# Loading and norming x in two groups around the first conditioning half, with the engines pinned in program order

## The chip, the cores and the metric

The kernel runs on one core of a Trainium2 chip. The metric is the time of one execution on the device, in microseconds; several runs are made and their median is given. One more execution is recorded by the profiler, and all positions below ("at 59.68") are microseconds from the start of the span in that record. The engines are TensorE (PE, with its weight loads as PEld), VectorE (DVE), ScalarE (ACT), GpSimd (POOL) and SyncE (SP), which here only issues transfers.

## The reference

One inference step of a small decoder trunk with two layers, width 1024, for a prompt of 1024 tokens and 8 single decode tokens. Each sub-layer normalises, modulates by a conditioning vector, runs a mixer or an FFN, and adds the gated result:

```python
def modulate(x, g, shift, scale):
    y = rms_norm(x, g) * (1.0 + scale[:, None, :]) + shift[:, None, :]
    return y.astype(x.dtype)

def ada_params(c, w, b):
    return (jax.nn.silu(c) @ w + b).astype(jnp.float32)

# in trunk(), for each layer l
sh1, sc1, g1, sh2, sc2, g2 = jnp.split(ada_params(c, w_ada[l], b_ada[l]), 6, axis=-1)
xn = modulate(h, norm_w[l, 0], sh1, sc1)
# layer 0: hgrn2_mixer(xn, ...), 8 heads, q, f_raw, i, g = split(xn @ w_in)
# layer 1: attention over a window of 128, with sinks and a shared K/V
h = h + g1 * mix
xn = modulate(h, norm_w[l, 1], sh2, sc2)
h = h + g2 * swiglu(xn, w_ffn_in[l], w_ffn_out[l])
```

So before the first product of layer 0 the kernel needs three things: the transposed input, the root mean square of each token, and the first 2048 columns of the conditioning product (shift and scale). All of it is float32.

## The kernel before

Activations lie transposed in SBUF: eight tiles `h[k]`, 128 features by 1024 tokens, and a small tile `hd` for the eight decode tokens. The 1032 tokens are cut into three chunks of 344 columns (grid `G3`). Every product in full precision is made of three matmuls on rounded float32 (`mm3`, lines 283 to 285): operands are split into a rounded high part and a low rest, and high by high, high by low and low by high are added in PSUM. A weight tile comes by a transfer into `raw` (line 195), ScalarE rounds it (line 182) and POOL subtracts to get the rest (line 185). For the first four units of weights this conversion is not run at once but kept in `held` and called by hand with `held.pop(0)()`.

The start, in the order in which it is written:

- SyncE loads the conditioning vectors, then the eight x blocks of 128 tokens (`load_x`, line 382), the first weight unit, eight row tiles of 512 KB of the first conditioning half (`first_half`, line 401), two more weight units, and then the second half.
- ScalarE squares and sums each x block (`first_square`, line 863). TensorE transposes the blocks in three groups (`turn_x`, line 455) and VectorE copies them into `h` (line 457).
- All nine columns of sums go through one reciprocal root (`newton`, lines 543 to 552). VectorE writes the results on diagonals (line 893), and TensorE spreads them over all partitions with a matrix of ones (line 909) into `N.R` (line 910).
- `first_step` (line 503) multiplies the conditioning vectors with the row tiles, eight steps for a half. `first_end` copies the sums (line 514), transposes them (line 517) and makes shift and scale (lines 522 and 523, and 530 in `mod_scale`). A half serves four of the eight feature tiles.
- `Norm.apply_steps` makes the input of the products: VectorE multiplies `h`, scale and `N.R` (line 740), ScalarE adds the shift and rounds (line 744), VectorE takes the rest (line 745).
- `hgrn_first` makes the four products of head 0. With the first half alone, parts of 12 matmuls over four feature tiles can run (`part(c, i)` for chunk `c`, unit `i`). Then come the second conditioning half, the applies that it frees, and the full products (288 matmuls in all). The written order has parts (0,0), (0,1), (0,2), (1,0), the eight steps of the second half, part (1,1), its end, and part (1,2).

PSUM has two pools of four banks, `mmp()` (mm) and `axp()` (ax). A tile with tag `c4` takes one of 34 slots in SBUF.

The order on each engine comes from a scheduler with a model of times. It may move an instruction ahead of others on its engine when it takes the inputs to be there. `tc.keep_in_program_order(i)` pins an instruction behind the one written before it on its engine. In the kernel before, only a few instructions are pinned. So the loads of the attention sinks (lines 1261 and 1266) and the copies of the K and V caches (lines 1269 and 1270), which are written in `biases()` and called in the middle of the first FFN, are issued within the first 65 us. `biases()` also negates the sinks on VectorE (line 1272, pinned).

Of the kernel before, what the change touches and what calls it, by code (L numbers as in the profile page):

```python
# [11 lines left out]
AF = mybir.ActivationFunctionType  # L12
ALU = mybir.AluOpType
# [4 lines left out]
P = 128  # L18
D = 1024
KT = 8  # L20
# [45 lines left out]
def trunk_kernel(  # L66
# [203 lines left out]
    def ada_unit(w, k, c0):  # L270
# [9 lines left out]
        ca.add(go)  # L280

    def mm3(ps, wh, wl, xh, xl, first, last):
        pe.matmul(ps, wh, xh, start=first, stop=False)  # L283
        pe.matmul(ps, wh, xl, start=False, stop=False)  # L284
        pe.matmul(ps, wl, xh, start=False, stop=last)  # L285

# [93 lines left out]
    def load_x(tb):  # L380
        t = big(cols=D)
        sp.dma_start(t, x_prompt[0, tb * P : (tb + 1) * P, :])
        xt.append(t)
# [10 lines left out]
    act.dma_start(pr2[56:57, :], gnorm_a)  # L394
    for tb in range(3, 8):
        load_x(tb)


# [7 lines left out]
    for kk in range(4):  # L406
        t = big(cols=1024)
        wa[0].append(first_half(2 * kk, 0, t))
        t = big(cols=1024)
        wa[0].append(first_half(2 * kk + 1, 0, t))  # L410
    ws.ahead(3)
    for k in range(4):
        t = big(cols=1024)
        wa[1].append(first_half(k, 1, t))

# [34 lines left out]
    dve.tensor_copy(hd, ps[:, : KT * NB].rearrange("p (k b) -> p k b", k=KT))  # L450
    def turn_x(t0, n):
        for k in range(KT):
            ps = mmp() if k % 2 else axp()
            for j in range(n):
                pe.transpose(ps[:, j * P : (j + 1) * P], xt[t0 + j][:, k * P : (k + 1) * P], ident)
            dst = h[k][:, t0 * P : (t0 + n) * P]
            dve.tensor_copy(dst, ps[:, : n * P])


# [22 lines left out]
    def ada_end(q):  # L482
# [7 lines left out]
        for b in range(4):  # L490
# [5 lines left out]
            )  # L496

    def first_step(i, k):
        if k == 0:
            ada_ps[0] = axp()  # L500
        for s in range(2):
            j = s + 2 * (k % 2)
            pe.matmul(
                ada_ps[0][32 * j : 32 * j + 32, :],
                cT[:, k, :],
                wa[i][k][:, s * 512 : (s + 1) * 512],
                start=(k < 2),
                stop=(k >= KT - 2),
                tile_position=(0, 32 * j),
            )  # L510

    def first_end(i):
        a = big(cols=512)
        act.copy(a, ada_ps.pop(0))
        ps = axp()
        for b in range(4):
            pe.transpose(ps[:, b * P : (b + 1) * P], a[:, b * P : (b + 1) * P], ident)
# [4 lines left out]
        dve.tensor_tensor(dst, psv[:, 0:2, :, 0:9], bc(bias, 3, 9), op=ALU.add)  # L522
        dve.tensor_tensor(dst, dst, psv[:, 2:4, :, 0:9], op=ALU.add)
        mod_scale(0, ks)

    MODS = {0: (0, 8, 0), 1: (24, 32, 8), 2: (96, 104, 32), 3: (48, 56, 16), 4: (72, 80, 24)}

    def mod_scale(m, ks=slice(0, KT)):
        _, sc, nw = MODS[m]
        dve.scalar_tensor_tensor(  # L530
            modA[:, m, ks, :],
            ada[:, sc : sc + KT, :][:, ks, :],
            1.0,
            bc(nT[:, nw : nw + KT][:, ks], 2, 9),
            op0=ALU.add,
            op1=ALU.mult,
        )
# [144 lines left out]
    class Norm:  # L682
# [50 lines left out]

        def apply_steps(self, c, m, x):
            sh = MODS[m][0]
            n, s = self.g.pl[c], self.g.prompt(c)
            for k in range(KT):
                xh, xl = (z[:, :n] for z in x.at(k, self.g, c))
# [123 lines left out]
    def first_square(tb):  # L862
        act.activation(junk[:, :T], xt[tb], AF.Square, accum_out=ms[:, tb : tb + 1])

    act.activation(junk[:NB, :T], xd_in, AF.Square, accum_out=ms[:NB, 8:9])
    for tb in range(3):
        first_square(tb)
    turn_x(0, 3)
    for tb in range(3, 6):
        first_square(tb)  # L870
    turn_x(3, 3)
    for tb in range(6, 8):
        first_square(tb)
    held.pop(0)()


# [11 lines left out]

    dve.tensor_scalar(ms, ms, 1.0 / D, EPS, op0=ALU.mult, op1=ALU.add)
    newton(y, ms, 9, P, "n")  # L890
    for half in range(2):
        s = slice(512 * half, 512 * half + 512)
        dve.tensor_tensor(
            dg[:, s].rearrange("p (j q) -> p j q", j=4),
            bc(ident, 1, 4),
            bc(y[:, 4 * half : 4 * half + 4], 2, P),
            op=ALU.mult,
        )
    dve.tensor_tensor(dg[:NB, T:TOK], ident[:NB, :NB], y[:NB, 8:9].to_broadcast([NB, NB]), op=ALU.mult)
    turn_x(6, 2)  # L900
    for k in range(4, KT):
        wa[1].append(first_half(k, 1, big(cols=1024)))
    ws.ahead(4)
    for k in range(2):
        first_step(0, k)
    for half in range(2):
        s = slice(512 * half, 512 * half + 512)
        ps = axp()
        pe.matmul(ps, ones, dg[:, s], start=True, stop=True)
        act.copy(N.R[:, s], ps)  # L910
    ps = axp()
    pe.matmul(ps[:, :NB], ones[:NB, :], dg[:NB, T:TOK], start=True, stop=True)
    act.copy(N.R[:, T:TOK], ps[:, :NB])
    for k in range(2, KT):
        first_step(0, k)
    first_end(0)
    X = Rows(KT)
    steps = [N.apply_steps(c, 0, X) for c in range(NCH)]
    held.pop(0)()
    for c in range(2):  # L920
        for _ in range(2):
            next(steps[c])
        if c == 0:
            held.pop(0)()
# [40 lines left out]
    def hgrn_first():  # L965
# [3 lines left out]
        def part(c, i):  # L969
            acc[c, i] = axp() if c and i < 2 else mmp()  # L970
            proj(acc[c, i][:, :W], us[i], X, c, 0, 4)

        for c, i in ((0, 0), (0, 1), (0, 2), (1, 0)):
            part(c, i)
        for k in range(KT):
            first_step(1, k)
        part(1, 1)
        first_end(1)
        part(1, 2)
        held.pop(0)()  # L980
        for st in steps:
            for _ in st:
                pass
        for _ in us:
# [258 lines left out]
    def biases():  # L1243
# [16 lines left out]
        sk = cst.tile([P, 16], F32, name="sk")  # L1260
        sp.dma_start(sk, sinks_b[0].partition_broadcast(P))
        skd = cst.tile([P, 1], F32, name="skd")
        late = cst.tile([P, 2 * P], F32, tag="early", name="late")
        biasd = late[:, 0:P]
        for b in range(NB):
            sp.dma_start(skd[16 * b : 16 * b + 16, :], sinks_b[0].unsqueeze(1))
            sp.dma_start(biasd[16 * b : 16 * b + 16, 1:P], rd[:, P : 2 * P - 1])
            sp.dma_start(biasd[16 * b : 16 * b + 16, 0:1], rd[:, 2 * P - 1 : 2 * P])
        sp.dma_start(ck_sample[:, 0 : WIN - 1], cache_swa_k[:, 1:WIN])
        sp.dma_start(cv_sample[:, 0 : WIN - 1], cache_swa_v[:, 1:WIN])  # L1270
        for t in (sk, skd):
# [788 lines left out]
```

## Time and profile before

| what | value |
|---|---|
| median of 3 runs | 2515.46 us (2510.66 to 2519.86) |
| time of the profiled execution | 2514.68 us |
| its span, first to last instruction | 2512.9 us |
| TensorE busy | 2462.7 us, 98% of the span |
| VectorE, ScalarE, POOL busy | 1388.1, 898.8, 789.8 us |
| mean granted TensorE clock | 0.993 |
| TensorE idle, waiting on a last conditioning row | 1.8 us ahead of 28.89 |
| first `mm3` matmul | at 39.42 |
| first matmul behind the second conditioning half | at 59.68 |

A line of a timeline reads: start, duration, engine, source line, operation, output and input tile names, shapes, count of merged instructions, and in brackets the idle time before it with what ended it. Tiles with tag `c4` are called `c`. Instructions of one engine can overlap by about a tenth of a microsecond, so the distance of two starts tells more of a stream's rate than a duration does.

### The profile page before, as it was taken

What the parts mean: (1) busy time and instruction counts of PE and PEld (TensorE: products, weight loads), DVE (VectorE), ACT (ScalarE), POOL (GpSimd) and SP (SyncE); (2) the same over time, 40 slices, a digit from 0 to 9 for tenths busy, and PEclk for the clock granted to TensorE, in tenths of its full rate; (3) what the DMA queues carried; (4) which work ended last, traced back from release to release, by engine and by line L of the source; (5) the groups of instructions that cost most, each with busy time, mean ns of one, the idle gap of its engine ahead of it and who ended that gap; (6) DMA issues with size and microseconds to landing.
All of it is one profiled execution on the core that took longest, in us unless ns stands there. A gap on an engine that the chain in (4) does not pass through costs nothing.

```text
span 2512.9 us, 52301 instructions
## 1 busy us (share of the span) xinstructions
PE 2462.7 (98%) x21531; PEld 2338.6 (93%) x21531; DVE 1388.1 (55%) x3153; ACT 898.8 (36%) x2003; POOL 789.8 (31%) x575
## 2 busy tenths in 40 slices
PE   7999999999999999999999999999999999999998
PEld 5999999987889999999999997878999999999998
DVE  5544544454587554656433735576875555565436
ACT  4433333331363332333211555454543333333112
POOL 1211111120325444544432130202254444445221
PEclk9999999999999999999999999999999999999999
DMA  8564222258942223226321322433222222264201
GB/s 313 194 207 147 73 80 70 76 150 269 289 126 85 78 85 120 89 84 233 127 71 56 93 56 60 140 105 110 76 85 77 76 77 77 76 236 144 68 26 68
DMA packets 314560, 293.41 MB, mean 117 GB/s; under 512 B 28681, under 2 KB 291738, under 8 KB 314290
## 3 DMA queue, kind: packets, MB, share of 16 engines
q1 hardware_dynamic: 313920, 289.86, 35.9%
q8 instruction: 169, 2.77, 0.5%
q14 instruction: 69, 0.57, 0.1%
q10 hardware_dynamic: 402, 0.22, 0.0%
HBM read 231.27 MB, written 63.99 MB: 117 GB/s over the span
## 4 chain that ended last, share of the span: by engine, by line
PE 90%; DVE 4%; DMA 2%; issue 2%; ACT 1%; SPq 0%; ACTq 0%; POOL 0%; DVEq 0%; POOLq 0%
PE mm L283 21%; PE mm L284 20%; PE mm L285 20%; PE ax L283 6%; PE ax L285 6%; PE ax L284 6%; PE ax L473 2%; PE ax L1806 1%; PE ax L1877 1%; PE ax L1045 1%; PE ax L1863 1%; PE ax L1135 1%; PE ax L1172 1%; PE ax L1171 0%; DMA gd<-rd 0%
## 5 line engine op out<-in xcount | busy, mean ns | idle before, releaser
L185 POOL TENSOR_TENSOR wu<-raw,wu 128x512 fp32r<-128x512 f32 x464 | 632.3, 1370 | 1429.5 <-ACT wu L182 1313.4
L283 PE MATMUL mm<-c,wu 128*128 128x344 f32 (+1 forms) x2096 | 670.3, 320 | 5.4 <-ACT c L744 4.3
L284 PE MATMUL mm<-c,wu 128*128 128x344 f32 (+1 forms) x2096 | 658.7, 314 | 0.1
L285 PE MATMUL mm<-c,wu 128*128 128x344 f32 (+1 forms) x2096 | 658.5, 314 | 0.0
L182 ACT CAST wu<-raw 128x512 fp32r<-128x512 f32 x464 | 285.5, 620 | 678.6 <-PE mm L285 363.7
L283 PEld LDWEIGHTS mm<-c,wu 128*128 128x128 f32 x2096 | 395.7, 189 | 18.5 <-issue 9.3
L284 PEld LDWEIGHTS mm<-c,wu 128*128 128x128 f32 x2096 | 396.1, 189 | 4.2 <-issue 3.4
L285 PEld LDWEIGHTS mm<-c,wu 128*128 128x128 f32 x2096 | 395.6, 189 | 2.5 <-issue 2.4
L283 PE MATMUL mm<-xq,wu 128*128 128x258 f32 x1376 | 391.3, 284 | 1.3 <-ACT wu L182 1.0
L285 PE MATMUL mm<-xq,wu 128*128 128x258 f32 x1376 | 389.6, 283 | 0.8 <-POOL wu L185 0.8
L284 PE MATMUL mm<-xq,wu 128*128 128x258 f32 x1376 | 389.9, 283 | 0.0
L283 PE MATMUL ax<-xq,wu 128*128 128x258 f32 x1120 | 316.7, 283 | 0.0
L285 PE MATMUL ax<-xq,wu 128*128 128x258 f32 x1120 | 316.3, 282 | 0.0
L284 PE MATMUL ax<-xq,wu 128*128 128x258 f32 x1120 | 316.1, 282 | 0.0
L283 PEld LDWEIGHTS mm<-xq,wu 128*128 128x128 f32 x1376 | 260.9, 190 | 2.7 <-ACT wu L182 1.2
L285 PEld LDWEIGHTS mm<-xq,wu 128*128 128x128 f32 x1376 | 261.0, 190 | 2.3 <-issue 1.2
L284 PEld LDWEIGHTS mm<-xq,wu 128*128 128x128 f32 x1376 | 261.8, 190 | 0.1
L846 DVE SCALAR_TENSOR_TENSOR hs<-mm,ada,hs 128x344 f32<-128x344 f32 (+3 forms) x228 | 120.6, 533 | 179.1 <-PE mm L285 170.4
L284 PEld LDWEIGHTS ax<-xq,wu 128*128 128x128 f32 x1120 | 212.0, 189 | 0.0
L283 PEld LDWEIGHTS ax<-xq,wu 128*128 128x128 f32 x1120 | 211.6, 189 | 0.0
L285 PEld LDWEIGHTS ax<-xq,wu 128*128 128x128 f32 x1120 | 211.3, 189 | 0.0
L846 DVE SCALAR_TENSOR_TENSOR c<-mm,ada,c 128x344 f32<-128x344 f32 (+1 forms) x132 | 75.0, 571 | 111.9 <-PE mm L285 111.7
(323 smaller groups left out, 3633.8 us busy)
## 6 DMA issues: line engine op xcount, KB each, us to landing
c<-in_w_ada_dram SPq DMA_DIRECT2D x96, 512.0 KB, 7.8
raw<-in_w_ffn_in_dram SPq DMA_DIRECT2D x160, 256.0 KB, 3.2
ff<-c SPq DMA_DIRECT2D x44, 516.0 KB, 2.7
c<-ff SPq DMA_DIRECT2D x44, 516.0 KB, 7.8
raw<-in_w_ffn_out_dram SPq DMA_DIRECT2D x44, 512.0 KB, 3.5
raw<-in_w_in_a_dram SPq DMA_DIRECT2D x32, 512.0 KB, 4.4
hs<-hs SPq DMA_DIRECT2D x16, 516.0 KB, 4.4
out_dram<-c SPq DMA_DIRECT2D x16, 512.0 KB, 3.3
```

The lines of the kernel that those rows point to most:

```text
L182: i = act.copy(u[:, 0, :], src)
L185: eng.tensor_tensor(u[:, 1, :], src, u[:, 0, :], op=ALU.subtract)
L283: pe.matmul(ps, wh, xh, start=first, stop=False)
L284: pe.matmul(ps, wh, xl, start=False, stop=False)
L285: pe.matmul(ps, wl, xh, start=False, stop=last)
L473: pe.matmul(ada_ps[q][32 * j : 32 * j + 32, 256 * i : 256 * i + 256], cT[:, k, :], u[i][:, j, :], start=(k == 0 and i == 0), stop=(k == KT ...
L846: dve.scalar_tensor_tensor(hc, ps[:, : g.pl[c]], ada[:, gate + n, 0:1], hc, op0=ALU.mult, op1=ALU.add)
L1045: pe.matmul(ps[32 * j : 32 * j + 32, c * 32 : (c + 1) * 32], KS[:, t0 : t0 + 32], QP[:, t0 : t0 + 32], start=True, stop=True, tile_positio ...
L1135: pe.matmul(ps[:, j * P : (j + 1) * P], kt[:, s], vt[:, s], start=True, stop=True)
L1172: pe.matmul(o, attT[:, c, :], vt[:, s], start=(c == 0), stop=True)
L1806: pe.matmul(psv[hf][:, gi, s0:256], q[2 * gp + gi][r, tb * P : (tb + 1) * P], kT[a][r, (tb - 1) * P + s0 : (tb + 1) * P], start=True, stop ...
L1863: pe.transpose(ps[:, g * P : (g + 1) * P], L[:, g, sb * P : (sb + 1) * P], ident)
```

## The change

The diff does five things.

1. Loading: only three x blocks are loaded ahead of the first conditioning half. The other five come after it and after the second weight unit. All eight row tiles of the second half are issued behind the fourth weight unit.
2. Norming in two groups: the first three blocks (384 tokens, enough for chunk 0) are squared, transposed, rooted and spread around the steps of the first half. The other five blocks and the decode column follow behind the first two parts of head 0, in `hgrn_first`. The copies of blocks 6 and 7 go to ScalarE.
3. Applying: for feature tiles 0 to 3, `first_scaled` multiplies `h` and `N.R` before shift and scale are known. `first_apply` then uses scale and shift at once on ScalarE, and on VectorE makes the unrounded value again and subtracts. Tiles 4 to 7 of chunk 0 go the same way; the rest still goes through `apply_steps`, with a new argument for the first tile.
4. Order: nearly every instruction of this stage on TensorE, ScalarE and VectorE is pinned (`fix`), the parts of head 0 by the flag `in_order`. The full products are not pinned. The parts are now (0,0), (0,1), then the second norm group, (0,2), (0,3), applies of chunk 1, (1,0), four steps of the second half, (1,1), four more steps, and the end of the half.
5. In `biases()` the sink loads and the cache copies are pinned on SyncE's queue, in the middle of the first FFN.

```diff
     def mm3(ps, wh, wl, xh, xl, first, last):
+        def put(i):
+            if in_order[0]:
+                tc.keep_in_program_order(i)
...
-    for tb in range(3, 8):
-        load_x(tb)
...
+    ws.ahead(2)
+    for tb in range(3, 8):
+        load_x(tb)
     ws.ahead(3)
-    for k in range(4):
-        t = big(cols=1024)
-        wa[1].append(first_half(k, 1, t))
...
+    fix = tc.keep_in_program_order
...
+    def turn(k, t0, n, ps, eng):
+        for j in range(n):
+            fix(pe.transpose(ps[:, j * P : (j + 1) * P], xt[t0 + j][:, k * P : (k + 1) * P], ident))
+        dst = h[k][:, t0 * P : (t0 + n) * P]
+        fix(eng(dst, ps[:, : n * P]))
+
+    def first_root(t0, n):
+        w = n + (t0 + n == 8)
+        v, yv = ms[:, t0 : t0 + w], y[:, t0 : t0 + w]
+        fix(dve.tensor_scalar(v, v, 1.0 / D, EPS, op0=ALU.mult, op1=ALU.add))
+        newton(yv, v, w, P, "n")
...
+        fix(dve.tensor_tensor(dgv, bc(ident, 1, n), bc(yv[:, :n], 2, P), op=ALU.mult))
...
+    def first_spread(s, parts=P):
+        ps = axp()
+        w = s.stop - s.start
+        fix(pe.matmul(ps[:, :w], ones[:parts], dg[:parts, s], start=True, stop=True))
+        fix(act.copy(N.R[:, s], ps[:, :w]))
+
+    def first_scaled(c, k):
+        t = small([P, W], "w", 6)
+        s = G3.prompt(c)
+        fix(dve.tensor_tensor(t[:, : G3.pl[c]], h[k][:, s], N.R[:, s], op=ALU.mult))
+        return t
+
+    def first_apply(c, k, t):
+        n = G3.pl[c]
+        xh, xl = (z[:, :n] for z in X.at(k, G3, c))
+        scale, shift = modA[:, 0, k, 0:1], ada[:, k, 0:1]
+        fix(act.activation(xh, t[:, :n], AF.Identity, scale=scale, bias=shift))
+        u = small([P, W], "w", 6)[:, :n]
+        fix(dve.tensor_scalar(u, t[:, :n], scale, shift, op0=ALU.mult, op1=ALU.add))
+        fix(dve.tensor_tensor(xl, u, xh, op=ALU.subtract))
...
     for tb in range(3):
         first_square(tb)
-    turn_x(0, 3)
-    for tb in range(3, 6):
-        first_square(tb)
-    turn_x(3, 3)
-    for tb in range(6, 8):
-        first_square(tb)
     held.pop(0)()
+    for k in range(KT):
+        turn(k, 0, 3, mmp() if k % 2 else axp(), dve.tensor_copy)
+        if k == 5:
+            first_root(0, 3)
+    ws.ahead(4)
+    for k in range(KT):
+        wa[1].append(first_half(k, 1, big(cols=1024)))
...
+    for k in range(6):
         first_step(0, k)
+    first_spread(slice(0, 3 * P))
+    for k in range(6, KT):
         first_step(0, k)
+    scaled = [first_scaled(0, k) for k in range(4)]
     first_end(0)
     X = Rows(KT)
+    for k in range(4):
+        first_apply(0, k, scaled[k])
+        if k == 1:
             held.pop(0)()
...
         def part(c, i):
-            acc[c, i] = axp() if c and i < 2 else mmp()
+            acc[c, i] = axp() if c else mmp()
+            in_order[0] = True
             proj(acc[c, i][:, :W], us[i], X, c, 0, 4)
-        for c, i in ((0, 0), (0, 1), (0, 2), (1, 0)):
-            part(c, i)
+            in_order[0] = False
+        part(0, 0)
+        part(0, 1)
+        for tb in range(3, 8):
+            first_square(tb)
+        held.pop(0)()
         for k in range(KT):
+            for t0, n in ((3, 3), (6, 2)):
+                turn(k, t0, n, axp(), act.copy if n == 2 else dve.tensor_copy)
+            if k == 1:
+                first_root(3, 5)
+        held.pop(0)()
+        part(0, 2)
+        for s in (slice(3 * P, 7 * P), slice(7 * P, T)):
+            first_spread(s)
+        first_spread(slice(T, TOK), NB)
+        part(0, 3)
+        for k in range(4):
+            first_apply(1, k, first_scaled(1, k))
+        part(1, 0)
+        for k in range(4):
             first_step(1, k)
         part(1, 1)
+        for k in range(4, KT):
+            first_step(1, k)
+        scaled = [first_scaled(0, k) for k in range(4, KT)]
         first_end(1)
-        part(1, 2)
-        held.pop(0)()
-        for st in steps:
-            for _ in st:
-                pass
+        for k in range(4, KT):
+            first_apply(0, k, scaled[k - 4])
+        for _ in N.apply_steps(1, 0, X, 4):
+            pass
+        for _ in N.apply_steps(2, 0, X):
+            pass
...
-        sp.dma_start(sk, sinks_b[0].partition_broadcast(P))
+        fix(sp.dma_start(sk, sinks_b[0].partition_broadcast(P)))
...
-            sp.dma_start(skd[16 * b : 16 * b + 16, :], sinks_b[0].unsqueeze(1))
+            fix(sp.dma_start(skd[16 * b : 16 * b + 16, :], sinks_b[0].unsqueeze(1)))
...
-        sp.dma_start(ck_sample[:, 0 : WIN - 1], cache_swa_k[:, 1:WIN])
-        sp.dma_start(cv_sample[:, 0 : WIN - 1], cache_swa_v[:, 1:WIN])
+        fix(sp.dma_start(ck_sample[:, 0 : WIN - 1], cache_swa_k[:, 1:WIN]))
+        fix(sp.dma_start(cv_sample[:, 0 : WIN - 1], cache_swa_v[:, 1:WIN]))
```

More of the change, by code (lines that the diff above doesn't have):

```diff
@@ L280, in ada_unit @@
         ca.add(go)
+    in_order = [False]
     def mm3(ps, wh, wl, xh, xl, first, last):
-        pe.matmul(ps, wh, xh, start=first, stop=False)
-        pe.matmul(ps, wh, xl, start=False, stop=False)
-        pe.matmul(ps, wl, xh, start=False, stop=last)
+        def put(i):
+            if in_order[0]:
+                tc.keep_in_program_order(i)
+        put(pe.matmul(ps, wh, xh, start=first, stop=False))
+        put(pe.matmul(ps, wh, xl, start=False, stop=False))
+        put(pe.matmul(ps, wl, xh, start=False, stop=last))
     def proj(ps, u, x, c, k0=0, k1=KT, g=G3):
@@ L450, in trunk_kernel @@
     dve.tensor_copy(hd, ps[:, : KT * NB].rearrange("p (k b) -> p k b", k=KT))
[L451 to L457, printed above, removed]
     ada = cst.tile([P, 112, 9], F32, name="ada")
@@ L502, in first_step @@
             j = s + 2 * (k % 2)
-            pe.matmul(
+            fix(pe.matmul(
                 ada_ps[0][32 * j : 32 * j + 32, :],
@@ L509, in first_step @@
                 tile_position=(0, 32 * j),
-            )
+            ))
     def first_end(i):
         a = big(cols=512)
-        act.copy(a, ada_ps.pop(0))
+        fix(act.copy(a, ada_ps.pop(0)))
         ps = axp()
         for b in range(4):
-            pe.transpose(ps[:, b * P : (b + 1) * P], a[:, b * P : (b + 1) * P], ident)
+            fix(pe.transpose(ps[:, b * P : (b + 1) * P], a[:, b * P : (b + 1) * P], ident))
         ks = slice(4 * i, 4 * i + 4)
@@ L521, in first_end @@
         bias = bT[:, 0:16].rearrange("p (s k) -> p s k", s=2)[:, :, ks]
-        dve.tensor_tensor(dst, psv[:, 0:2, :, 0:9], bc(bias, 3, 9), op=ALU.add)
-        dve.tensor_tensor(dst, dst, psv[:, 2:4, :, 0:9], op=ALU.add)
-        mod_scale(0, ks)
+        fix(dve.tensor_tensor(dst, psv[:, 0:2, :, 0:9], bc(bias, 3, 9), op=ALU.add))
+        fix(dve.tensor_tensor(dst, dst, psv[:, 2:4, :, 0:9], op=ALU.add))
+        fix(mod_scale(0, ks))
     MODS = {0: (0, 8, 0), 1: (24, 32, 8), 2: (96, 104, 32), 3: (48, 56, 16), 4: (72, 80, 24)}
@@ L529, in mod_scale @@
         _, sc, nw = MODS[m]
-        dve.scalar_tensor_tensor(
+        return dve.scalar_tensor_tensor(
             modA[:, m, ks, :],
@@ L732, in finish, with apply_steps @@
             act.copy(self.R[:, s], ps[:, :w])
-        def apply_steps(self, c, m, x):
+        def apply_steps(self, c, m, x, k0=0):
             sh = MODS[m][0]
             n, s = self.g.pl[c], self.g.prompt(c)
-            for k in range(KT):
+            for k in range(k0, KT):
                 xh, xl = (z[:, :n] for z in x.at(k, self.g, c))
@@ L862, in first_square @@
     def first_square(tb):
-        act.activation(junk[:, :T], xt[tb], AF.Square, accum_out=ms[:, tb : tb + 1])
-    act.activation(junk[:NB, :T], xd_in, AF.Square, accum_out=ms[:NB, 8:9])
+        fix(act.activation(junk[:, :T], xt[tb], AF.Square, accum_out=ms[:, tb : tb + 1]))
+    def turn(k, t0, n, ps, eng):
[3 more added lines that the diff above has]
+        fix(eng(dst, ps[:, : n * P]))
@@ new lines, in first_root @@
+    def first_root(t0, n):
[3 more added lines that the diff above has]
+        newton(yv, v, w, P, "n")
+        s = slice(t0 * P, (t0 + n) * P)
+        dgv = dg[:, s].rearrange("p (j q) -> p j q", j=n)
+        fix(dve.tensor_tensor(dgv, bc(ident, 1, n), bc(yv[:, :n], 2, P), op=ALU.mult))
+        if w > n:
+            dgd = dg[:NB, T:TOK]
+            fix(dve.tensor_tensor(dgd, ident[:NB, :NB], y[:NB, 8:9].to_broadcast([NB, NB]), op=ALU.mult))
@@ L866, in trunk_kernel @@
+    fix(act.activation(junk[:NB, :T], xd_in, AF.Square, accum_out=ms[:NB, 8:9]))
     for tb in range(3):
         first_square(tb)
-    turn_x(0, 3)
-    for tb in range(3, 6):
-        first_square(tb)
-    turn_x(3, 3)
-    for tb in range(6, 8):
-        first_square(tb)
-    held.pop(0)()
+    held.pop(0)()
+    for k in range(KT):
[5 more added lines that the diff above has]
+        wa[1].append(first_half(k, 1, big(cols=1024)))
@@ L887, in trunk_kernel @@
     dve.tensor_scalar(omlb, lb, -1.0, 1.0, op0=ALU.mult, op1=ALU.add)
[L889 to L904, printed above, removed]
-        first_step(0, k)
[L906 to L914, printed above, removed]
+    for k in range(6):
+        first_step(0, k)
+    first_spread(slice(0, 3 * P))
+    for k in range(6, KT):
         first_step(0, k)
+    scaled = [first_scaled(0, k) for k in range(4)]
     first_end(0)
     X = Rows(KT)
-    steps = [N.apply_steps(c, 0, X) for c in range(NCH)]
-    held.pop(0)()
[L920 to L923, printed above, removed]
+    for k in range(4):
+        first_apply(0, k, scaled[k])
+        if k == 1:
             held.pop(0)()
```

1 line of the change is left out of this document (removed).

## The prediction

> **What bounds the kernel now.** I read the page first, then the busy time by stretches, then the chain of waits, then the timelines of the first 65 us engine by engine. The page and the stretches (columns: busy time and instruction count of PE, PEld, DVE, ACT, POOL, then granted clock, DMA share, GB/s):
>
> ```profile
> PE 2462.7 (98%) x21531; PEld 2338.6 (93%) x21531; DVE 1388.1 (55%) x3153; ACT 898.8 (36%) x2003; POOL 789.8 (31%) x575
> ```
> ```profile
> 29.00:30.00 1.00, 1.00 (x4) 0.07 (x4) 0.00 (x0) 0.00 (x0) 0.00 (x0) 0.50 1.10 335
> ...
> 130.00:2512.00 2382.00, 2348.76 (x20474) 2243.45 (x20472) 1319.73 (x3001) 843.47 (x1890) 761.77 (x546) 0.99 0.34 109
> ```
>
> TensorE is the bound. From 130 us on it is busy for 2348.8 of 2382 us, so a lead won or lost before that travels to the end nearly one for one. What the change can move is the start, where TensorE waits. The chain of waits there:
>
> ```profile
> 28.89 3.23 PE ax L503 x8
> ...
> 34.82 0.50 ACT c L514
> ...
> 36.58 0.64 DVE modA L530
> ...
> 38.78 0.59 ACT c L744
> 39.42 0.94 PE mm L283 x2
> ```
>
> and TensorE's timeline:
>
> ```profile
> 21.99 1.05 PE L503 MATMUL ax<-c,cT 128*32 128x512 f32 x4 [0.27 <-DMA c<-in_w_ada_dram]
> ...
> 44.73 0.49 PE L284 MATMUL mm<-c,wu 128*128 128x344 f32 x1
> 45.02 0.49 PE L285 MATMUL mm<-c,wu 128*128 128x344 f32 x1
> ...
> 47.62 0.32 PE L285 MATMUL mm<-c,wu 128*128 128x344 f32 x1
> 47.78 0.32 PE L283 MATMUL mm<-c,wu 128*128 128x344 f32 x1
> ...
> 50.23 4.17 PE L503 MATMUL ax<-c,cT 128*32 128x512 f32 x32
> ...
> 59.68 0.74 PE L283 MATMUL mm<-c,wu 128*128 128x344 f32 x3 [0.87 <-ACT c L744]
> ```
>
> The last weight row of the first conditioning half lands at 28.89, and the first three-part product starts at 39.42. A matmul of 344 columns then costs 0.29 us (44.73 to 45.02) and, once the clock is back, 0.16 us (47.62 to 47.78). The line that decides is the last: at 59.68, when the second conditioning half is through, 72 of the 288 matmuls of the first head are done (parts of 12: chunk 0 for three units, chunk 1 for three units). The new order also has done 72 of 288 there (chunk 0 for four units, chunk 1 for two). What remains is the same 216 matmuls. So the change is worth the difference of that one moment, which I call the resume.
>
> **The loads.** SyncE issues in order:
>
> ```profile
> 1.88 7.25 SPq L382 DMA_DIRECT2D c<-in_x_prompt_dram  x8
> ...
> 9.65 9.09 SPq L401 DMA_DIRECT2D c<-in_w_ada_dram  x8
> ...
> 32.27 6.99 SPq L1266 DMA_DIRECT2D skd<-in_sinks_b_dram  x8
> 39.30 0.83 SPq L1269 DMA_DIRECT2D out_dram<-in_cache_swa_k_dram  x1
> ```
>
> Before, 8 blocks of x, one weight tile and 8 conditioning rows of 512 KB each come first, so row 7 is the 17th transfer. Now it is 3 + 1 + 8 = the 12th. In the trace the 12th is row 2 of the same half, which TensorE took up when it landed at 21.99. I take 21.99 for row 7: 6.9 us sooner than 28.89. One place in that order is (28.89 − 21.99)/5 = 1.4 us, which is my error on it. Blocks 3 to 7 are the 14th to 18th and land at 24.7 to 30.2; the third weight tile, the 19th, at 31.6. Rows of the second half end as the 28th at about 44, before they are wanted. The eight sink loads (7.0 us of issue) and the cache copies no longer stand in that queue at 32 to 40; this is worth nothing by itself, since TensorE shows no DMA wait ahead of 50.23, and their new place is a rival below.
>
> **The first products.** The last row's matmuls end by 22.9 (0.13 each in the 50.23 row, 0.40 in the 28.89 row; four of them, 0.9 taken). From the copy of the sums to the end of the modulation took 34.82 to 37.22 = 2.4 us, with 0.1 to start it: 25.5. The scaling by the norm is now done ahead, in cover of the last rows, so ScalarE applies at once (0.59) and TensorE starts near 26.2, 13.2 us sooner than 39.42. If the scaling is late, each of its four steps costs up to 0.5 us here.
>
> **What now stands between.** ScalarE and VectorE got work into this place that before lay ahead of the last row, where both were waiting anyway:
>
> ```profile
> 17.64 1.06 ACT L863 ACTIVATE c<-c 128x1024 f32<-128x1024 f32 x1
> ...
> 18.82 1.06 ACT L863 ACTIVATE c<-c 128x1024 f32<-128x1024 f32 x1
> ...
> 35.18 1.16 ACT L182 CAST wu<-raw 128x512 fp32r<-128x512 f32 x2
> ...
> 59.04 1.56 ACT L744 ACTIVATE c<-w,ada 128x344 fp32r<-128x344 f32 x3 [2.79 <-DVE w L740]
> ```
> ```profile
> 20.57 2.50 POOL L185 TENSOR_TENSOR wu<-raw,wu 128x512 fp32r<-128x512 f32 x2 [18.80 <-ACT wu L182]
> ...
> 41.91 2.92 POOL L185 TENSOR_TENSOR wu<-raw,wu 128x512 fp32r<-128x512 f32 x2 [2.64 <-ACT wu L182]
> ```
> ```profile
> 18.99 0.55 DVE L457 COPY c<-mm 128x384 f32<-128x384 f32 x1
> ...
> 21.11 0.76 DVE L889 TENSOR_SCALAR nms<-nms 128x9 f32<-128x9 f32 x1
> ...
> 22.11 0.98 DVE L543 TENSOR_SCALAR nt<-nms 128x9 int32<-128x9 int32 x1
> ...
> 23.35 0.16 DVE L546 TENSOR_SCALAR ny<-nt 128x9 int32<-128x9 int32 x1
> ...
> 25.64 0.69 DVE L893 TENSOR_TENSOR c<-ident,ny 128x512 f32<-128x512 f32 x1
> ...
> 42.09 1.60 DVE L740 SCALAR_TENSOR_TENSOR w<-c,modA,c 128x344 f32<-128x344 f32 x1
> ```
>
> ScalarE, pinned: four applies at about 0.5 with one pair of casts (1.16) between, from 25.5 to 28.7. Then five squares at 1.18 (17.64 to 18.82): 5.9 us, to 34.6. Then the casts of the third unit, to 35.8.
>
> VectorE beside it: while POOL subtracts, its SBUF work stretches. The 42.09 row took 1.60 us for what takes half a microsecond elsewhere, under the POOL row of 41.91, and L889 and L543 ran 0.76 and 0.98 under the POOL row of 20.57, where L546, alone, took 0.16. The subtractions of the second unit (27.2 to 29.8) therefore fall on the applies of chunk 0 and cost about 1.3 us; the 24 matmuls of the first two parts end near 34.0 (DVE-paced, then partly at 0.29).
>
> The root of the other five blocks waits for the squares (34.6) and, in VectorE's order, for two turned copies (35.5). POOL subtracts the third unit from 35.3 to 37.9, on top of the root's first two steps, as at 20.57. Ten further small steps near 0.2 (23.35 to 25.64 before, with a few others in between) and a diagonal of 640 columns (0.69 for 512, so about 0.9, and 0.1 for decode): 40.8. Only then do VectorE's six copies of the remaining turned rows come, and each row needs its PSUM bank back. On TensorE a row is five transposes:
>
> ```profile
> 13.74 0.85 PE L455 MATMUL ax<-ident,c 128*128 128x128 f32 x3
> 14.38 0.85 PE L455 MATMUL mm<-ident,c 128*128 128x128 f32 x3
> ```
>
> Three took 0.64 at the slow clock, so five take 1.07; at the full clock, by the ratio 0.16/0.29, 0.59. Four rows cannot run ahead (four banks hold the first two and the third row's halves), so the turning ends between 41.4 + 4 × 0.55 = 43.6 and 41.4 + 4 × 1.07 = 45.7. TensorE has been nearly idle from 35 to 41, as from 27 to 28.9 before, after which the clock row reads 0.50. I take the slow side, 45.
>
> The Trainium skill's page "TensorE: Matmul & The Clock Gate", section "Why this matters for your kernels", says to leave no idle gap above about 3 us between bursts of matmuls, or the clock halves. By that rule the new gap costs the 2.1 us between those ends, and without it the resume below would come at 63.6. The 0.50 row agrees with it.
>
> The page "SBUF — State Buffer", section "Who interferes with whom", says a GpSimd instruction that reads SBUF blocks a VectorE one with two SBUF inputs, or in a 2-port mode, for its whole length. The 1.60 row agrees; by the rule alone the collisions would cost what I counted.
>
> **From the turning to the resume,** all in pinned order: part of unit 2 (12 matmuls, 1.9 to 3.5, 2.4 taken); the first spread 0.6; its copy 0.7 with the start; then chunk 1's four rows, each scale 0.5, apply 0.6, subtract 0.5 in a ring, 1.65 with two hand-overs, 6.6 in all, while unit 3's part lies beside the first; the last three matmuls 0.5; second-half steps 4.2 (the 50.23 row); one more part 1.9; and the end of the half, 0.1 + 2.4 + 0.6 = 3.1. Sum 20.0, so the resume is at 45 + 20 = 65.0, against 59.68: 5.3 us later. The 13 us won ahead is spent on a chain that TensorE could not fill. From the profiled execution's 2514.68 us that is 2520.0. The median of the runs is 2515.46, 0.8 above that execution, and I leave it there.
>
> Bounds. Best: row 7 one place sooner, no POOL collision, full clock: turning ends at 39.5, tail 18.9, resume 58.4, 1.3 us early: 2513.4. Worst: turning 46.5, tail 21.5, resume 68: 2523.0. A later schedule that falls otherwise can add some us either way: the idle time behind 130 us is 33 us in all, and I allow a fifth of it, 6 us. The remaining edits (shared helper returning its instruction, starting row argument) issue the same work and cost nothing; the extra spread and root are about 16 small instructions, counted above.
>
> **Rivals.** *Slower: the late sinks stall VectorE.* The eight loads and two copies now go among the bias loads in the middle of the first FFN:
>
> ```profile
> 945.07 0.13 DVE L1272 TENSOR_SCALAR skd<-skd 128x1 f32<-128x1 f32 x1
> ```
> ```profile
> 948.45 1.94 SPq L1267 DMA_DIRECT2D late<-rd  x1
> ...
> 963.78 0.42 SPq L1268 DMA_DIRECT2D late<-rd  x1
> ```
> ```profile
> 967.66 0.42 DVE L1501 TENSOR_TENSOR c<-c,mm 128x258 f32<-128x258 f32 x1 [3.38 <-PE mm L285]
> ...
> 970.47 0.42 DVE L1506 TENSOR_TENSOR c<-c,mm 128x258 f32<-128x258 f32 x1 [0.94 <-PE mm L285]
> ```
>
> The last sink would be issued about 7 us after 963.8, at 971. If the sign flip keeps its place at 945, VectorE stands 26 us with all PSUM reads queued behind it. TensorE has 8 banks and fills two in each 2.8 us, so 11 us is hidden and 15 us shows: 2535. It decides from a stall of 11 us on. Against it: the flip may be queued after its loads, and then it costs nothing. 1 in 11.
>
> *Slower: the start itself costs over 7.5 us,* with the worst bound and a poor later schedule, about 2525. 4 in 25.
>
> *Faster: the pins fill TensorE.* If nothing but work stood between 26.2 and the resume (72 matmuls 11.3, 40 transposes 4.7, conditioning 4.2, spreads and end 3, slow clock 2.6), the resume would be at 52: 2507. For it speaks the early start; against it the squares, which cannot end before 31.5 with block 7 landing at 30.2. 1 in 10.
>
> *Nothing changes:* the gain ahead and the waits behind cancel, 2515 (down to 2508). 17 in 100.
>
> **How the numbers follow.** My case, 0 to 7.5 us later, has 48 in 100. About 0.3% (7.5 us) is what a measurement of this kernel tells from no change; so "same" is 0.48 + 0.17 = 0.65, slower 0.16 + 0.09 = 0.25, faster 0.10. The range, 2509 to 2530, takes in the bounds with the 6 us and leaves out the filled TensorE and the 15 us stall; my own case alone spans 2515 to 2523.
>
> **What would show it.** The first L283-line matmul near 26; row 7's wait ending near 22; five squares from about 28.7; a TensorE gap with clock 0.50 between 34 and 45, released by VectorE's copies; resume near 65. I am wrong if the turning is through before 39, if the clock stays at 1.00 there, or if VectorE shows a DMA wait on the sinks near 950.

## The result and the profile after

| | before | after |
|---|---|---|
| median of 20 runs each | 2514.49 us (2509.98 to 2519.86) | 2522.07 us (2517.77 to 2529.17) |
| time of the profiled execution | 2514.68 us | 2518.70 us |
| its span | 2512.9 us | 2516.9 us |
| first `mm3` matmul | 39.42 | 26.15 |
| resume (first matmul behind the second conditioning half) | 59.68 | 64.54 |

The ratio of the times is 1.0032, 95% interval 1.0025 to 1.0038: the changed kernel is about 8 us slower. The profiled execution shows 4.0 us of that, the resume 4.9. The page's line on the engines, and the stretches of the first 70 us and the long one behind (busy time of PE, PEld, DVE, ACT, POOL, then granted clock, DMA share, GB/s), of the changed kernel:

```profile
PE 2464.7 (98%) x21533; PEld 2339.8 (93%) x21533; DVE 1394.1 (55%) x3169; ACT 903.5 (36%) x2012; POOL 790.7 (31%) x575
```
```profile
20.00:30.00 10.00, 6.76 (x25) 2.87 (x21) 7.61 (x18) 5.61 (x11) 2.75 (x2) 0.81 1.06 396
30.00:40.00 10.00, 9.17 (x42) 7.68 (x42) 4.58 (x17) 7.21 (x15) 3.47 (x4) 0.68 1.07 390
40.00:50.00 10.00, 8.44 (x49) 6.93 (x49) 6.41 (x16) 4.51 (x11) 2.51 (x2) 1.00 1.05 368
50.00:60.00 10.00, 8.56 (x41) 4.11 (x45) 4.83 (x11) 1.34 (x2) 0.00 (x0) 0.83 0.77 300
60.00:70.00 10.00, 7.69 (x55) 6.13 (x48) 6.87 (x22) 5.85 (x16) 0.00 (x0) 1.00 0.00 0
...
130.00:2512.00 2382.00, 2352.76 (x20573) 2247.68 (x20565) 1327.75 (x3005) 845.52 (x1894) 764.06 (x547) 1.00 0.34 110
```

From 20 to 70 TensorE is busy for 40.6 of 50 us, but the mean clock is 0.81 and 0.68 in the first two stretches: much of the "busy" there is matmuls at half speed. Behind 130 it idles for 29 us, against 33 before, so no new waits were bought there. TensorE's timeline of the changed kernel shows where the time is (brackets: idle time before, and what ended it):

```profile
21.42 1.85 PE L500 MATMUL ax<-c,cT 128*32 128x512 f32 x8
...
26.15 0.65 PE L289 MATMUL mm<-c,wu 128*128 128x344 f32 x1 [1.52 <-ACT c L900]
...
30.50 0.66 PE L290 MATMUL mm<-c,wu 128*128 128x344 f32 x1 [1.53 <-DVE c L903]
...
36.00 3.76 PE L865 MATMUL ax<-ident,c 128*128 128x128 f32 x25
...
41.57 1.88 PE L865 MATMUL ax<-ident,c 128*128 128x128 f32 x12 [0.80 <-DVE c L867]
43.21 0.40 PE L289 MATMUL mm<-c,wu 128*128 128x344 f32 x1
...
51.51 0.42 PE L289 MATMUL ax<-c,wu 128*128 128x344 f32 x1 [0.55 <-ACT c L900]
...
53.20 0.46 PE L289 MATMUL ax<-c,wu 128*128 128x344 f32 x1 [0.55 <-ACT c L900]
...
54.62 3.01 PE L500 MATMUL ax<-c,cT 128*32 128x512 f32 x16
...
59.64 1.92 PE L500 MATMUL ax<-c,cT 128*32 128x512 f32 x16
...
64.54 0.88 PE L289 MATMUL mm<-c,wu 128*128 128x344 f32 x4 [1.58 <-ACT c L900]
```

Read from the top: the last two rows of the first half (21.42) are in without a wait; the products begin at 26.15, 13.3 us sooner than before; two parts run at half clock until the turning of the second group begins at 36.00; the turning ends at 43.21; then chunk 1's applies pace TensorE in steps of 1.69 us (51.51 to 53.20); the second half's steps follow, half of them at the low clock (3.01 against 1.92 for the same sixteen); and at its end TensorE waits again (1.58) before the full products resume. The 13 us are gone by then, and 5 more.

### The profile page after: what moved, and what is told of

Its sections match the earlier page's. It is cut to its first block, busy times and chain, and to the rows that moved or that the text cites. A ratio compares the mean times of both kernels' runs of the same rounds, so it can differ in the third digit from the quotient of the medians.

```text
span 2516.9 us, 52338 instructions
## 1 busy us (share of the span) xinstructions
PE 2464.7 (98%) x21533; PEld 2339.8 (93%) x21533; DVE 1394.1 (55%) x3169; ACT 903.5 (36%) x2012; POOL 790.7 (31%) x575
## 4 chain that ended last, share of the span: by engine, by line
PE 90%; DVE 4%; DMA 3%; issue 1%; ACT 1%; SPq 0%; POOL 0%; DVEq 0%; ACTq 0%; POOLq 0%
PE mm L289 20%; PE mm L291 20%; PE mm L290 20%; PE ax L289 6%; PE ax L291 6%; PE ax L290 6%; PE ax L468 2%; PE ax L1847 1%; PE ax L1918 1%; PE ax L1086 1%; PE ax L1904 1%; PE ax L1176 1%; DMA raw<-in_w_ffn_in_dram 1%; PE ax L1213 1%; PE ax L1212 0%
```

## The experiments

"Resume" is always the first full product behind the second conditioning half, "head 0" the first transpose of head 0's core, which comes behind all 288 products (96.0 before, 100.6 after). Ratios are against runs of the kernel before on the same chip.

**The two kernels once more.** Is one profile of a start typical?

> The kernel before once more, for a second profile of its start. Theory A (the run with late sinks gained by a free queue): first product again at 39 to 40 and resume at 59 to 60.5. Theory B (it gained by the phase of the clock or by jitter of the transfers): one of the two differs by over 1.5 us from the first profile, towards 37 and 56.

> The changed kernel once more, for a second profile of its start. If the start is settled by the pinned order, the resume is again between 64 and 65.5, and what the span differs from 2516.9 lies behind 130 us. If the phase of the clock sets the start, the resume moves by over 1.5 us.

The kernel before a second time (2516.11 us), TensorE:

```profile
37.05 0.94 PE L283 MATMUL mm<-c,wu 128*128 128x344 f32 x2 [3.41 <-ACT c L744]
...
50.50 1.05 PE L503 MATMUL ax<-c,cT 128*32 128x512 f32 x4 [0.20 <-DMA c<-in_w_ada_dram]
51.82 1.05 PE L503 MATMUL ax<-c,cT 128*32 128x512 f32 x4 [0.27 <-DMA c<-in_w_ada_dram]
...
57.96 0.74 PE L283 MATMUL mm<-c,wu 128*128 128x344 f32 x3 [0.69 <-ACT c L744]
```

The changed kernel a second time (2519.30 us):

```profile
26.21 0.42 PE L289 MATMUL mm<-c,wu 128*128 128x344 f32 x1 [1.52 <-ACT c L900]
...
41.46 2.90 PE L865 MATMUL ax<-ident,c 128*128 128x128 f32 x12 [1.64 <-DVE c L867]
...
65.65 0.89 PE L289 MATMUL mm<-c,wu 128*128 128x344 f32 x4 [1.58 <-ACT c L900]
```

So the resume of the kernel before is 59.68 or 57.96, that of the changed one 64.54 or 65.65. In the first profile of before, the wait for a conditioning row was 1.78 us ahead of 28.89 and the clock fell there; here the longest such wait is 0.5 us, the clock stays at 1.00 until 35, and the first product comes 2.4 us sooner. The profile on which the prediction rests was the slower of these two starts. The positions moved as theory B had it, so the place of one resume cannot show what an edit of a few microseconds is worth. The changed kernel met neither of its two cases: its resume moved by 1.1 us, out of the 64 to 65.5 and by less than the 1.5. The loss at the resume is 4.9 to 7.7 us, not one number. Head 0 stands at 94.3 and 101.7 in these profiles.

**The late sinks alone.** The kernel before, with only the fifth part of the change (the eight loads and the two cache copies like the first):

```diff
+        fix = tc.keep_in_program_order
-        sp.dma_start(sk, sinks_b[0].partition_broadcast(P))
+        fix(sp.dma_start(sk, sinks_b[0].partition_broadcast(P)))
...
```

> The kernel before, with only the sink loads and cache copies pinned late. Start-chain theory (the 5 us are lost between 26 and 65 us): same as before, within 2 us, and the first matmul behind the second conditioning half stays near 59.7. Late-sinks rival: 4 to 8 us slower, with the loss in the first FFN near 950 to 990.

2509.57 us, ratio 0.9983 (0.9975 to 0.9992): faster by about 4 us, against what I expected. SyncE's queue and the resume, first in the second profile of the kernel before, then with the sinks late:

```profile
30.86 7.02 SPq L1266 DMA_DIRECT2D skd<-in_sinks_b_dram  x8
...
38.80 2.53 SPq L401 DMA_DIRECT2D c<-in_w_ada_dram  x4
```
```profile
31.84 8.11 SPq L401 DMA_DIRECT2D c<-in_w_ada_dram  x4
```
```profile
37.05 0.94 PE L283 MATMUL mm<-c,wu 128*128 128x344 f32 x2 [3.41 <-ACT c L744]
...
47.33 3.64 PE L503 MATMUL ax<-c,cT 128*32 128x512 f32 x32
...
56.11 0.74 PE L283 MATMUL mm<-c,wu 128*128 128x344 f32 x3 [0.74 <-ACT c L744]
```

The two executions are nearly twins up to the second half's steps (first product 37.05 in both, steps begun at 47.32 and 47.33). Then the last eight matmuls wait for rows that were issued behind the sinks, from 38.80 instead of 31.84, and the resume is 57.96 against 56.11. This is 1.85 us of the queue, shown in one pair of executions. They stay as far apart at head 0 (94.3 and 92.5) and at the same conversion on POOL near 306 (307.77 and 305.87). What the ratio holds beyond that, 4 us in its middle and 2 at its lower end, these profiles do not show.

**The sinks early in the changed kernel.** The same edit undone there (`fix` taken off these loads).

> The changed kernel with the eight sink loads and the two cache copies unpinned again, so that they are issued in the first 70 us as before; nothing else differs. Theory A (the sink loads block the queue of the start for 7 us of issue, and taking them out is worth about 4 us in any order of the start): slower than the changed kernel by 2 to 5 us, that is 2524 to 2527, resume 66 to 69. Theory B (in the changed order the second conditioning half has landed long before it is wanted, so the place of the sinks is worth nothing, and the gain of the late sinks in the kernel before came from its own order or from the phase of the clock): resume 64 to 65 and 2520 to 2524, level with the changed kernel. I lean to B, 60 in 100.

2527.76 us, ratio to before 1.0047 (1.0031 to 1.0064): slower than with the sinks late by near 6 us in the medians and near 4 in the ratios, whose intervals overlap (1.0025 to 1.0038 there). Theory A comes nearer in time, though for the most part not by its place: the resume is only 0.5 to 1.7 us later than in the two profiles of the changed kernel (66.19), and head 0 is 2.1 to 3.2 us later, at 103.8. By the first matmul of line 1212 this profile is 11.6 us behind the first one of the changed kernel (169.1 against 157.5), so over 8 us arise between: behind the first transpose the scheduler put the instructions in another order. TensorE's busy time and waits in that place:

```profile
130.00:140.00 10.00, 6.18 (x246) 4.15 (x245) 5.54 (x12) 1.14 (x3) 0.00 (x0) 1.00 0.67 218
```
```profile
134.90 0.72 PE L1086 MATMUL ax<-c,c 128*32 128x32 f32 x62 [1.07 <-DVE c L1108]
...
141.42 1.06 PE L468 MATMUL ax<-c,cT 128*32 128x256 f32 x3 [3.13 <-issue]
```

A chain of small matmuls and VectorE steps that other products cover in the changed kernel (where TensorE is busy for all 10 us from 130 to 140) lies bare here. Why the scheduler ordered it so was not tried. The three ratios fit together: start alone 1.0047, sinks alone 0.9983, product 1.0030, measured for both 1.0032. By them the new start with the order that follows from it costs about 12 us (8 to 16 by the interval), and the late sinks give about 4 back (2 to 6). But that order behind head 0 is not the changed kernel's, so these 12 us are not what the start costs there. At head 0 the run with the sinks early is 7.8 to 9.5 us behind the kernel before, the changed kernel 4.6 to 7.4.

**The steps of the second half sooner.** The changed kernel, with four steps ahead of part (1,0):

```diff
-        part(1, 0)
         for k in range(4):
             first_step(1, k)
+        part(1, 0)
         part(1, 1)
```

> The changed kernel, with the first four steps of the second half moved ahead of part (1,0) on TensorE. If the ring scale, apply, subtract of chunk 1 is what holds TensorE from 48.7 to 54.6, the steps cover it and the resume comes 2.5 to 3.5 us sooner, near 61.3; the time falls to about 2519. If the ring only hides another wait (the last rows of the half, the copies), the resume stays at 64.5.

2518.17 us, ratio 1.0016 (1.0007 to 1.0025); resume:

```profile
60.99 0.89 PE L289 MATMUL mm<-c,wu 128*128 128x344 f32 x4 [1.59 <-ACT c L900]
```

3.6 us sooner than after, as expected; head 0 is at 97.0. Half of the loss is that TensorE stood in the ring of chunk 1's applies while ready work was queued behind it in pinned order.

**The ring and the end of the half covered.** On top of that, chunk 1's four scales in a row, and parts (1,1) and (1,2) laid into the end of the second half, one behind its copy and one behind its transposes:

```diff
+        scaled = [first_scaled(1, k) for k in range(4)]
         for k in range(4):
-            first_apply(1, k, first_scaled(1, k))
+            first_apply(1, k, scaled[k])
...
-        first_end(1)
+        first_end(1, lambda: part(1, 1), lambda: part(1, 2))
```

> The changed kernel with steps_ahead, with the four scales of chunk 1 made in a row, and with part (1,1) and a further part (1,2) laid beside the end of the second half, as before the change. Start-chain theory: the two uncovered waits (ring 4 us, end of the half 3 us) go; the resume, with 84 instead of 72 matmuls done, comes near 60, which is 6 us better than the changed kernel, about level with the kernel before. Otherwise the loss lies elsewhere and the time stays near 2522.

2514.02 us, ratio 1.0001 (0.9992 to 1.0011): level with the kernel before. The resume comes at 59.27 with 84 matmuls done, near the 60 expected, and head 0 at 93.6. TensorE's last wait ahead of the resume:

```profile
52.59 0.43 PE L290 MATMUL ax<-c,wu 128*128 128x344 f32 x1 [0.22 <-DVE c L907]
```

From 53 to 66 it is busy for all 13.0 us, against 10.4 in the changed kernel. So the waits between 46 and 64 are as much as the net loss. Against the kernel before with the sinks late, which shares that part of the change, this version is still slower: 1.0001 against 0.9983, about 4 us, of which head 0 shows 1.1 (93.6 against 92.5). Where the others lie is not shown.

**The root behind the turned copies.** The prediction had the root hold up the turning; here it comes behind all eight rows.

```diff
-            if k == 1:
-                first_root(3, 5)
+        first_root(3, 5)
```

> The changed kernel, with the root of the second group behind all turned copies on VectorE, and not behind the first two. If the root (37.7 to 41.1) is what held the six copies back, the turning ends near 40.3 instead of 43.2, and the resume comes 1.5 to 2 us sooner. If TensorE's slow clock paces the turning, it ends where it did, and the later root costs up to 2 us.

2524.67 us, ratio 1.0038 (1.0026 to 1.005). The turning, begun 0.5 us later at 36.48, ended at 43.2 as in the changed kernel and not near 40.3; its first 18 transposes took 3.29 us, 0.18 each, and the mean clock from 35 to 40 was 0.75 against 0.86. The spread then waited:

```profile
40.43 2.76 PE L865 MATMUL ax<-ident,c 128*128 128x128 f32 x22 [0.65 <-DVE c L867]
...
48.93 3.00 PE L886 MATMUL ax<-c,ones 128*128 128x512 f32 x6 [3.84 <-DVE c L880]
...
67.86 1.21 PE L289 MATMUL mm<-c,wu 128*128 128x344 f32 x4 [1.59 <-ACT c L900]
```
```profile
44.29 1.20 DVE L548 TENSOR_TENSOR nt<-nt,nms 128x6 f32<-128x6 f32 x1
45.53 1.19 DVE L549 SCALAR_TENSOR_TENSOR ny<-nt,ny 128x6 f32<-128x6 f32 x1
```

My expected gain of 1.5 to 2 us was wrong: the turning did not become shorter by the root's time, and the root (3.3 us in the changed kernel, 37.74 to 41.05) is not saved, only moved. In its new place only part (0,2), 2 us, stands beside it, and two of its steps met POOL's subtractions, 1.2 us each instead of 0.17.

**The clock kept up.** Eleven unread matmuls of 128 columns (three, then eight) put into the waits at the end of the first half.

> The changed kernel with 11 unneeded matmuls of 128 columns on TensorE around the end of the first half (22.9 to 26.2), whose result nobody reads. Clock theory: the granted clock stays at 1.00 through 26 to 36, part (0,1) takes 1.9 instead of 3.5 us, resume 2 to 3 us sooner. If VectorE under POOL's subtractions paces this stretch, or if the clock falls anyhow, under 1 us.

2528.91 us, ratio 1.0055 (1.0041 to 1.0069), resume at 64.38. The stretches:

```profile
25.00:30.00 5.00, 3.18 (x19) 2.13 (x17) 4.50 (x8) 4.69 (x9) 2.90 (x3) 0.94 1.05 390
30.00:35.00 5.00, 4.55 (x15) 4.11 (x16) 1.53 (x3) 4.91 (x10) 0.82 (x1) 0.50 1.01 337
```

The clock read 0.94 instead of 0.61 from 25 to 30, and then 0.50 from 30 to 35 as before: it fell a few microseconds later, in the stretch that VectorE paces. The start gained nothing; the span's 9.6 us more lie behind the resume. About 3 of them arise before 150 and 6 between 1420 and 1940, where the clock reads 0.50 for some 3 us from 125, from 1538 and from 1654 on, as it does not in the changed kernel's profile; why is not settled.

**POOL's conversion.** The changed kernel with the conversion of the second unit behind all four applies instead of two:

```diff
     for k in range(4):
         first_apply(0, k, scaled[k])
-        if k == 1:
-            held.pop(0)()
+    held.pop(0)()
```

> The changed kernel with the conversion of the second weight unit behind all four applies of chunk 0 instead of between them. If POOL's subtractions hold VectorE there (1.42 and 1.41 us for steps of 0.5), part (0,0) ends near 30 instead of 32.5 and part (0,1) 1 to 2 us sooner than 36.0; the resume gains at most as much, since POOL then meets the root. If not, no move.

2521.14 us, ratio 1.0029 (1.0018 to 1.0039), resume 64.70: no difference. The collision only moved to the next tile:

```profile
31.72 0.65 PE L290 MATMUL mm<-c,wu 128*128 128x344 f32 x1 [1.94 <-DVE c L903]
```

**Scaling ahead alone.** The kernel before with only the third part of the change, for chunk 0's tiles 0 to 3.

> The kernel before with one part of the change alone: for the first four tiles of chunk 0 the product of h and the norm is made ahead, and ScalarE applies scale and shift at once. The first product starts 1 to 2 us sooner than 39.42; nothing else stands between, so the resume comes 0.5 to 2 us sooner than 59.7: 2513 to 2514. If the pins hurt the scheduler's order more, slower than before.

2515.52 us, ratio 1.0002 (0.9993 to 1.0011). The first product came at 36.06, against 39.42 and 37.05, and the gain went at once:

```profile
38.43 2.31 DVE L930 TENSOR_SCALAR w<-w,modA,ada 128x344 f32<-128x344 f32 x1
```
```profile
43.77 0.43 PE L284 MATMUL mm<-c,wu 128*128 128x344 f32 x1 [3.11 <-DVE c L931]
...
59.80 0.74 PE L283 MATMUL mm<-c,wu 128*128 128x344 f32 x3 [0.73 <-ACT c L744]
```

VectorE's step of 0.45 us took 2.31 beside a subtraction and a memset of POOL (38.29 to 40.55), and TensorE waited 3.11 us for the chain behind it.

**Late sinks and scaling ahead together,** with POOL's conversion of the second unit moved ahead of the end of the first half:

> The kernel before with the sinks and cache copies late, and with the product of h and N.R made ahead of shift and scale for the four tiles of chunk 0, as the change does it; the subtractions of the second unit are put ahead of the end of the first conditioning half, where POOL is idle. Theory (the 3.11 us wait in the run with scaling ahead alone was the collision with POOL and took back the 3.4 us that the early first product won): first product 33 to 35, no wait over 1.5 us up to 45, resume 53 to 56, time 2506 to 2509. Rival (the second conditioning half lands when it lands, and chunk 1's applies and the weights bound the resume): resume 56 to 57, time 2509 to 2511, as with the late sinks alone. Rival (POOL meets the newton root or the scaling instead): resume 58 or later and 2512 or more. 40, 40 and 20 in 100.

2510.53 us, ratio 0.9987 (0.9978 to 0.9997): faster than before, but no more than the late sinks alone. First product and resume:

```profile
38.08 0.94 PE L283 MATMUL mm<-c,wu 128*128 128x344 f32 x2 [1.83 <-ACT c L929]
...
59.27 0.74 PE L283 MATMUL mm<-c,wu 128*128 128x344 f32 x3 [0.74 <-ACT c L744]
```

There was no wait over 1.5 us from 38.08 to 45, as the theory said, but its first product, its time and its resume failed. The casts of the second unit, moved ahead with the subtractions, stand on ScalarE before the copy of the sums (1.15 us at 33.91), and TensorE waited 1.95 us for that copy instead of 0.92. This execution had the late conditioning row again (a wait of 1.81 us ahead of 29.06) and a clock of 0.54 from 40 to 45, and its 2514.03 us is the second longest of the eleven runs, so its resume doesn't speak for the median. The first rival has the time right, the second the resume. Whether the early first product is worth anything with the sinks late isn't settled by one such profile.

**The edits together** (steps sooner, ring and end covered, root last, conversion later):

> covered together with root_last and pool_later. Start-chain theory: 8 to 10 us better than the changed kernel, 2512 to 2514, slightly better than the kernel before. If the waits only move, no better than covered.

2518.81 us, ratio 1.0018 (1.0006 to 1.0029), 5 us over the covered version; the spread waited 3.84 us for the root again, at 47.56.

Two versions beat both kernels: the kernel before with late sinks (0.9983), and that with scaling ahead beside it (0.9987), which do not differ measurably.

## Why the prediction was right, and where only in sum

The time was put at 2520.0 us with a resume of 65.0; the profiled execution after took 2518.70 with 64.54, the median is 2522.07. The mechanism held: a lead of 13 us at the first product, spent on squares, root, turning and applies in pinned order. That the resume fits to half a microsecond is luck in part: the first two parts ended 2.0 us later than said, the turning still ended 1.8 us sooner than said, and the way from there to the resume took 1.3 us more. By its steps:

- **First products:** 26.2 said, 26.15 measured. Row 7 was in sooner than the 21.99 taken (no wait ahead of 21.42), and two rows ran in a block of 1.85 us. The prediction read 28.89 as the last row of the kernel before; that line has eight matmuls, two rows, so the wait was for the last but one.
- **Squares:** from 28.7 to 34.6 said. ScalarE in the changed kernel:

```profile
28.74 1.04 ACT L860 ACTIVATE c<-c 128x1024 f32<-128x1024 f32 x1
...
34.50 1.12 ACT L182 CAST wu<-raw 128x512 fp32r<-128x512 f32 x2
```

- **Parts (0,0) and (0,1):** 34.0 said, 36.0 measured. The collision with POOL came, on three steps that took 1.42, 1.41 and 0.79 us for 0.45 to 0.52; that is 2.2 us, where I had counted 1.3. And all matmuls behind it ran at 0.29 us, where I let the later ones run faster:

```profile
27.54 1.42 DVE L902 TENSOR_SCALAR w<-w,modA,ada 128x344 f32<-128x344 f32 x1
29.04 1.41 DVE L903 TENSOR_TENSOR c<-w,c 128x344 fp32r<-128x344 f32 x1
```
```profile
27.25 2.83 POOL L185 TENSOR_TENSOR wu<-raw,wu 128x512 fp32r<-128x512 f32 x2 [10.44 <-ACT wu L182]
```

- **Root:** ended at 40.8 said, 41.05 measured, by another way. It waited for TensorE's two turned rows instead of the squares, began just behind POOL's subtractions (35.18 to 37.68), and so was not stretched:

```profile
36.72 1.10 DVE L867 COPY c<-ax 128x384 f32<-128x384 f32 x2 [4.95 <-PE ax L865]
37.74 0.16 DVE L873 TENSOR_SCALAR nms<-nms 128x6 f32<-128x6 f32 x1
```

- **Turning:** 45 said, 43.2 measured. I had TensorE idle and slow from 35 to 41. It was busy to 39.7 and the clock was back: 25 transposes took 3.76 us, 0.15 each against 0.21 in the slow row of the prediction. The fast end, 43.6, was the right one here. The sign that I had named, a gap at a clock of 0.50, did not come: the two waits (0.46 and 0.80 us) fell in a stretch at 1.00, which I had named as a sign against me. In the second profile the sign did come, with a wait of 1.64 us for VectorE ahead of 41.46, a mean clock of 0.66 from 40 to 45 and the end at 44.0. So the slow clock there is a matter of the execution, and one profile could not confirm or refute that step. The other condition against me, a turning through before 39, came in neither.
- **Turning to resume:** 20.0 said, 21.3 measured. The ring's 1.69 per tile against 1.65 was right. Mis-sized were the steps (4.9 us for the two blocks instead of 4.2) and the ring with its last matmuls (46.86 to 54.62, 7.8 instead of 7.1), and the clock fell again near the end of the ring, in which TensorE is partly idle: sixteen steps took 3.01 us where the other sixteen took 1.92 (3.13 and 1.92 in the second profile).
- **The late sinks:** "worth nothing by itself" was wrong, by about 4 us (2 to 6 by the interval). I argued from TensorE's waits in one profile. There the slow first half had moved the second half's steps back until the rows issued behind the sinks were in; in the second profile they were waited for.
- **The rival of the sign flip** was rightly held unlikely. SyncE, the flip and TensorE in the first FFN after the change:

```profile
972.28 0.42 SPq L1307 DMA_DIRECT2D skd<-in_sinks_b_dram  x1
```
```profile
L1313 DVE TENSOR_SCALAR skd<-skd x1: 150/150/150, 988.9 to 988.9; 128x1 f32<-128x1 f32 x1
```
```profile
980.00:990.00 10.00, 10.00 (x86) 10.00 (x85) 5.06 (x14) 1.22 (x3) 0.00 (x0) 1.00 0.50 174
990.00:1000.00 10.00, 8.00 (x65) 7.57 (x64) 5.95 (x8) 4.96 (x10) 8.13 (x6) 1.00 0.33 99
```

The last sink is issued at 972, the flip has moved to 989, and TensorE does not stop up to 990. The 2.0 us that it stands behind that are no loss by the change: the kernel before stands 1.8 us from 980 to 990.

- **The sum:** +5.3 us against +7.6 in the medians, which is the edge between my case and the rival of a dearer start; the interval, 0.25 to 0.38%, has the 0.3% inside. I had under-counted the cost of the start and put the gain of the late sinks at nothing, and the two errors offset each other by luck: at head 0 the start without the late sinks costs 7.8 to 9.5 us, with them 4.6 to 7.4. One part of the first is the base: 59.68 was the later of two resumes of the kernel before. Where the other few microseconds lie stays open. Both profiled executions after (2518.70 and 2519.30 us) lie below the median of 2522.07, and the three runs over 2524 have a mean granted clock of 0.988 to 0.990 against 0.992 in the profiled ones, so some of it may be clock lost behind the start. In the profiles of both kernels the clock reads 0.50 for some 3 or 7 us at places that differ from one execution to the next (near 548, 1421, 1531 and 1797 in the first profile of the kernel before, near 546, 570, 1645 and 1798 in the second); which of them the three long runs had is not on record.

The Trainium skill's page "TensorE: Matmul & The Clock Gate", section "HAM oscillation — how this bites in real kernels", gives the rule as no idle gaps beyond about 3.4 us. Here the clock fell near 53.5 with listed waits of 0.51 to 0.55 us and TensorE busy for 3.56 of the 5 us from 50 to 55. So the traces do not agree with the rule as a safe limit. The 0.50 row of the kernel before, which the prediction called in agreement, does not agree either: the wait ahead of it was 1.78 us. Nor do short gaps always cost the clock: in the run with POOL's conversion later the same ring had the same waits, TensorE was busy for 3.13 of those 5 us, and the clock stayed at 1.00 (sixteen steps in 1.92 us behind it). What decides between the two is not shown.

## What to carry to other kernels

An early start of one engine is worth only what the engine can do until the next thing it must wait for; look at the waits before the steady part, and put ready work of other chains into them (here steps of the second half and parts of other units), since instructions pinned in order cannot fill them by themselves. Small transfers of no hurry can stand in a queue ahead of wanted rows: count their issue time even when one profile shows no wait, and take a second profile before a few microseconds are argued from one.

## What was not expected of the hardware

- Two executions of the same kernel differ by 2.4 us at the first product (39.42 and 37.05), since a row of 512 KB, the same transfer in the same queue, kept TensorE waiting 1.78 us in one and at most 0.5 in the other, and the clock behind it was 0.77 from 30 to 35 in the one and 1.00 in the other.
- Eight sink loads of about 0.1 KB each took 7.02 us to issue, and the stretch from 35 to 40 moved 159 GB/s in that profile, against 368 with the sinks late.
- VectorE steps on six columns took 1.2 us instead of 0.17 beside POOL's subtractions, and a 0.45 us step took 2.31 beside a subtraction and a memset: in these cases the stretch went by what POOL had in hand, not by the step's own size.
- Eleven filler matmuls delayed the clock's fall (0.94 from 25 to 30) but did not prevent it (0.50 from 30 to 35).
